# The causal mask of an attention block: a select on POOL after the sigmoid, in place of a product on PE before it

## The chip, the core and the metric

The kernel runs on one core of one Trainium2 chip. The time is the device time in microseconds from the launch's start to its end. PE is TensorE, ACT ScalarE, DVE VectorE, POOL GpSimd, and SP SyncE, which here only issues transfers. Each engine executes its own queue in order; a semaphore makes one engine wait for another.

## The reference, cut to what matters

One layer of a hybrid encoder: a projection, then stick-breaking attention (8 heads) beside an RWKV-7 recurrence, then an output projection and a feed-forward part, for 2048 prompt tokens and 32 sample tokens. The change is in the attention of the prompt:

```
z = q k^T / sqrt(64)                       # one row for each query t, one column for each key s
mask = s < t                               # strictly causal
log_1mb = where(mask, log_sigmoid(-z), 0)  # a masked key breaks nothing off: factor 1
after = reverse cumsum(log_1mb) - log_1mb
weight = where(mask, exp(log_sigmoid(z) + after), 0)
o = weight @ v
```

A key's weight is its sigmoid times the product of (1 - sigmoid) over all later keys before the query. A masked key must count as a factor of one in the running product.

## The kernel before

The kernel has three parts. The first projects all tokens and writes queries, keys and values to DRAM. The second, from about 943 to 1756 us of the profiled span, runs attention, recurrence and the first rows of the output projection interleaved. The third is the rest of the output projection and the feed-forward part.

Attention goes head by head, for each of four query blocks of 512 tokens (`qg`), through key blocks of 512 (`kc`) from the query's own block back to the first. In each pair of blocks there are four tiles of 128 queries (`j`). `scores` (lines 818 to 830) makes one tile: two products add up to the scores `z` in PSUM (queries and keys are split in a high and a low part), and in the query's own block, where `kc == qg`, only the first `n = (j + 1) * 128` keys are taken. The last 128 of these are the diagonal square. There a third product (line 827) adds `identr` times `mnegr`, that is 0 or -2^100, so that masked scores become hugely negative. `stick` (774 to 778) then makes the tile `R` in SBUF: a sigmoid of -z/8 on ACT gives the factor of each key, which is 1 where the score was masked, and a scan on DVE turns it, from the last key to the first, into running products. The scan takes its starting value from the key block treated before, and 1.0 in the own block. The scan's second operand is `z`, which it ignores, so a score buffer is free again only after the scan; there are three (`psZ`).

`turn` (832) transposes a tile's four squares on PE and splits them in high and low parts on ACT and DVE (`split`, line 103). `values` (844) multiplies them with differences of the values, which are held so that the running products can serve as weights. Transposes come four score tiles behind, and values two steps behind them.

The generators `attention`, `recurrence` and `first_rows` are drawn from by a loop with weights (line 1169), and a scheduling layer then sets each engine's order. POOL does little in this part: memsets of a recurrence tile (line 1028), powers and products of the group norm (983 to 989), and low parts of the output projection's operands (747). Each stands in POOL's queue and waits there for what it needs.

In this program 128 tiles have the mask product: 8 heads, 4 query blocks, 4 tiles each. The mask's constants are made once, at the start of part one (lines 92 to 94 and 180 to 185).

Of the kernel before, what the change touches and what calls it, by code (L numbers as in the profile page):

```python
# [10 lines left out]
F32R = mybir.dt.float32r  # L11
AF = mybir.ActivationFunctionType
ALU = mybir.AluOpType
# [4 lines left out]
P = 128  # L18
# [34 lines left out]
def kernel(ctx: ExitStack, tc: tile.TileContext, x_prompt, x_sample, cache_k, cache_v,  # L53
# [6 lines left out]
    PE, ACT, DVE, POOL, SP = nc.tensor, nc.scalar, nc.vector, nc.gpsimd, nc.sync  # L60
# [25 lines left out]
    ident = const.tile([P, P], F32, name="ident")  # L86
# [2 lines left out]
    POOL.memset(neghalf, -0.5)  # L89
    cab = ctx.enter_context(ExitStack())  # L90
    cp_ab = cab.enter_context(tc.tile_pool(name="cab", bufs=1))
    identr = cp_ab.tile([P, P], F32R, name="identr")
    POOL.tensor_copy(identr, ident)
    mnegr = cp_ab.tile([P, P], F32R, name="mnegr")
    mnegs = cp_ab.tile([P, TS], F32, name="mnegs")
    zr = cp_ab.tile([TS, 1], F32, name="zr")
    POOL.memset(zr, 0.0)
# [16 lines left out]
    with tc.tile_pool(name="pa0", bufs=1) as pe, tc.tile_pool(name="pa1", bufs=1) as pa, \  # L114
# [65 lines left out]
        mneg = pe.tile([P, MX + 2], F32, tag="df", name="mneg")[:, 0:P]  # L180
        POOL.memset(mneg, NEG)
        POOL.affine_select(mneg, mneg, [[1, P]], ALU.is_ge, 0.0, base=0, channel_multiplier=-1)
        POOL.tensor_copy(mnegr, mneg)
        for j in range(4):
            POOL.tensor_copy(mnegs[32 * j:32 * j + 32, :], mneg[0:32, 0:32])
        m64 = pe.tile([P, MX], mybir.dt.bfloat16, name="m64")
# [2 lines left out]
        for r in (0, 64):  # L189
            POOL.affine_select(mA[r:r + 64, 0:64], mA[r:r + 64, 0:64], [[1, 64]], ALU.is_gt, 0.0,  # L190
                               base=0, channel_multiplier=-1)
            POOL.affine_select(mA[r:r + 64, 64:128], mA[r:r + 64, 64:128], [[1, 64]], ALU.is_ge, 0.0,
                               base=0, channel_multiplier=-1)
# [69 lines left out]
        def superblock(sb, T0, NTILE):  # L263
# [154 lines left out]
            def g_k(w, c):  # L418
# [47 lines left out]
                def stage3(av, E65, Em, nrm):  # L466
                    rr = live["rr"]
                    kk = pe.tile([P, MX], F32, tag="kk", name="kk")
                    DVE.scalar_tensor_tensor(kk[:, 0:WT], kr[:, 0:WT], col(R_KK + c), nrm[:, 0:WT],
                                             ALU.mult, ALU.mult)  # L470
                    KB = pe.tile([P, 12, P], F32, tag="KB", name="KB")
                    QR = pe.tile([P, 12, P], F32, tag="QR", name="QR")
                    POOL.tensor_tensor(QR[:, 0:NC, 0:64], c3(kk), E65[:, 0:NC, 0:64], ALU.mult)
                    POOL.tensor_tensor(QR[:, 0:NC, 64:128], c3(rr), E65[:, 0:NC, 1:65], ALU.mult)
                    POOL.tensor_tensor(kk[:, 0:WT], kk[:, 0:WT], av[:, 0:WT], ALU.mult)
                    POOL.tensor_tensor(KB[:, 0:NC, 64:128], c3(kk), c3(Em), ALU.mult)
                    DVE.tensor_scalar(av[:, 0:WT], av[:, 0:WT], -1.0, col(R_KA + c), ALU.add, ALU.mult)
                    DVE.scalar_tensor_tensor(kr[:, 0:WT], av[:, 0:WT], 1.0, kr[:, 0:WT], ALU.add, ALU.mult)
                    POOL.tensor_tensor(KB[:, 0:NC, 0:64], c3(kr), c3(Em), ALU.mult)
                    DVE.scalar_tensor_tensor(rr[:, 0:WT], rr[:, 0:WT], col(R_RK + c), kr[:, 0:WT],  # L480
                                             ALU.mult, ALU.mult)
                    chunk_dst(lambda a, m: QR_d[a:a + m, c].rearrange("j p t -> p j t"), 0, NC,
                              lambda o, m: QR[:, o:o + m, :])
                    defer(3, lambda: scores(rr, KB, QR))
# [278 lines left out]
    with tc.tile_pool(reuse_waits="tile", name="bp", bufs=6) as bp, \  # L763
# [7 lines left out]
            tc.tile_pool(reuse_waits="tile", name="psX", bufs=1, space=PSUM) as psX:  # L771
        NB, LAG, LAG2, LOOK, RW = 12, 4, 2, 8, PAST + TS + 1

        def stick(z, R, n, before):

            ACT.activation(R[:, 0:n], z[:, 0:n], AF.Sigmoid, scale=-0.125)  # L776
            rv = R[:, 0:n][:, ::-1]
            DVE.tensor_tensor_scan(rv, rv, z[:, 0:n], before, ALU.mult, ALU.bypass)  # L778

# [8 lines left out]
        pieces, state = {}, {}  # L788
# [29 lines left out]
        def scores(h, qg, kc, j):  # L818

            k = pieces[h, kc][0]  # L820
            n = (j + 1) * P if kc == qg else 512
            z = psZ.tile([P, 512], F32, tag="z", name="z")
            js = slice(j * P, (j + 1) * P)
            PE.matmul(z[:, 0:n], state[h, qg][:, 0, js], k[:, 0:n], start=True, stop=False)  # L824
            PE.matmul(z[:, 0:n], state[h, qg][:, 1, js], k[:, 0:n], start=False, stop=kc != qg)  # L825
            if kc == qg:
                PE.matmul(z[:, n - P:n], identr, mnegr, start=False, stop=True)
            R = bk.tile([P, 512], F32, tag="R", name="R", bufs=NB)
            stick(z, R, n, 1.0 if kc == qg else state[h, qg, kc + 1, j][:, 0:1])
            state[h, qg, kc, j] = R  # L830

        def turn(h, qg, kc, kb):
# [91 lines left out]
        def attention():  # L924
            A, B, loads = [], [], []
            for hq, h in [(hq, h) for hq in range(2) for h in range(H)]:
                if hq == 0 and h == 2:
                    for kc in (2, 1, 0):
                        for e in range(2):
                            A.append((lambda kc=kc, e=e: s_scores(kc, e), 1.0 if kc == 2 else 3.0))  # L930
                        for e in range(2):
                            B.append((len(A) - 1, lambda kc=kc, e=e: s_turn(kc, e),
                                      lambda kc=kc, e=e: s_values(kc, e), 0.2 if kc == 2 else 2.0))
                for qg in (2 * hq, 2 * hq + 1):
                    for kc in range(qg, -1, -1):
                        loads.append((len(A), h, qg, kc))
                        for j in range(4):
                            n = (j + 1) * P if kc == qg else 512
                            A.append((lambda h=h, qg=qg, kc=kc, j=j: scores(h, qg, kc, j), 2 * n / 2400))
                        for kb in range(4):  # L940
                            m = 4 - (kb if kc == qg else 0)
                            B.append((len(A) - 1, lambda h=h, qg=qg, kc=kc, kb=kb: turn(h, qg, kc, kb),
                                      lambda h=h, qg=qg, kc=kc, kb=kb: values(h, qg, kc, kb),
                                      m * (0.107 + 2 * P / 2400)))
# [243 lines left out]
    with tc.tile_pool(reuse_waits="tile", name="c1", bufs=1) as cp, tc.tile_pool(reuse_waits="tile", name="psM", bufs=6, space=PSUM) as psM, \  # L1188
# [38 lines left out]
        with tc.tile_pool(reuse_waits="tile", name="co", bufs=2) as co:  # L1227
# [7 lines left out]
            for at, (i, dhs) in enumerate(tiles):  # L1235
                t0, n = halves[1][0][i]
# [20 lines left out]
        with tc.tile_pool(reuse_waits="tile", name="cz", bufs=3, side="right") as cz, \  # L1257
# [87 lines left out]
            for q in range(1, len(seq), 2):  # L1345
# [14 lines left out]
                hf, j = seq[q]  # L1360
# [31 lines left out]
```

## Time and profile before

| | us |
|---|---|
| median of 3 runs | 3440.98 (3435.89 to 3441.1) |
| the profiled execution | 3431.45 |
| its span, first to last instruction | 3429.6 |
| PE busy | 3258.3 (95%) |
| DVE busy | 1752.8 (51%) |
| ACT busy | 1151.4 (34%) |
| POOL busy | 861.8 (25%) |

The granted clock of PE averages 0.979 of 2.4 GHz. The busy shares are means over all three parts; what the change does has to be read in the second part alone, from 943 to 1756 us. A PE matmul's duration in a row is its run from first input to last output; the next one starts well before it ends.

### The profile page before, as it was taken

What the parts mean: (1) busy time and instruction counts of PE and PEld (TensorE: products, weight loads), DVE (VectorE), ACT (ScalarE), POOL (GpSimd) and SP (SyncE); (2) the same over time, 40 slices, a digit from 0 to 9 for tenths busy, and PEclk for the clock granted to TensorE, in tenths of its full rate; (3) what the DMA queues carried; (4) which work ended last, traced back from release to release, by engine and by line L of the source; (5) the groups of instructions that cost most, each with busy time, mean ns of one, the idle gap of its engine ahead of it and who ended that gap; (6) DMA issues with size and microseconds to landing.
All of it is one profiled execution on the core that took longest, in us unless ns stands there. A gap on an engine that the chain in (4) does not pass through costs nothing.

```text
span 3429.6 us, 50515 instructions
## 1 busy us (share of the span) xinstructions
PE 3258.3 (95%) x20281; PEld 2829.6 (83%) x20281; DVE 1752.8 (51%) x2449; ACT 1151.4 (34%) x2231; POOL 861.8 (25%) x719
## 2 busy tenths in 40 slices
PE   8998898889689999999999999999999999999998
PEld 7988898878677777877877989999899788888886
DVE  4675757678678888777853322222222322222223
ACT  6444343434155555454542311111112211111111
POOL 3332423253101121122223411212112321221121
PEclk9999999989889999999999999999999999999999
DMA  4555565565775655656643611111112411111111
GB/s 148 164 158 149 169 185 140 155 190 146 213 187 146 178 149 154 171 145 162 160 123 117 197 38 50 44 43 50 37 50 72 151 50 50 45 48 43 49 43 50
DMA packets 481762, 395.82 MB, mean 115 GB/s; under 512 B 72228, under 2 KB 403568, under 8 KB 481528
## 3 DMA queue, kind: packets, MB, share of 16 engines
q1 hardware_dynamic: 393000, 346.58, 35.5%
q10 hardware_dynamic: 88528, 46.02, 4.9%
q8 instruction: 160, 2.62, 0.3%
q14 instruction: 74, 0.61, 0.1%
HBM read 278.19 MB, written 114.31 MB: 114 GB/s over the span
## 4 chain that ended last, share of the span: by engine, by line
PE 50%; DVE 1%; DMA 0%; ACT 0%; issue 0%; POOL 0%; POOLq 0%; ACTq 0%; SPq 0%; DVEq 0%
PE gu L1305 29%; PE dn L1325 15%; PE mo L760 3%; PE wt L837 0%; PE pt L1221 0%; PE av L851 0%; PE av L852 0%; DVE R L778 0%; PE z L824 0%; PE sap L1104 0%; PE z L825 0%; PE snp L1113 0%; DMA mx<-mixT_d 0%; ACT yt L1213 0%; PE yp L1126 0%
## 5 line engine op out<-in xcount | busy, mean ns | idle before, releaser
L1328 DVE TENSOR_TENSOR x<-x,dn 128x512 f32<-128x512 f32 x374 | 255.7, 687 | 243.3 <-PE dn L1325 243.3
L778 DVE TENSOR_TENSOR_SCAN R<-R,z 128x512 f32<-128x512 f32 (+2 forms) x320 | 338.5, 1084 | 73.3 <-ACT R L776 70.8
L1305 PE MATMUL gu<-h2h,wh 128*128 128x352 f32 (+1 forms) x1760 | 368.4, 351 | 1.7 <-ACT wh L104 1.2
L1305 PE MATMUL gu<-h2h,wl 128*128 128x352 f32 (+1 forms) x1760 | 369.0, 351 | 0.0
L1305 PE MATMUL gu<-h2l,wh 128*128 128x352 f32 (+1 forms) x1760 | 367.3, 351 | 0.0
L1305 PEld LDWEIGHTS gu<-h2h,wh 128*128 128x128 f32 x1760 | 305.1, 188 | 33.9 <-ACT wh L104 1.4
L1305 PEld LDWEIGHTS gu<-h2l,wh 128*128 128x128 f32 x1760 | 305.3, 188 | 31.0
L1305 PEld LDWEIGHTS gu<-h2h,wl 128*128 128x128 f32 x1760 | 305.1, 188 | 30.2
L1325 PE MATMUL dn<-dh,hdh 128*128 128x512 f32 x748 | 295.1, 394 | 0.0
L1325 PE MATMUL dn<-dh,hdl 128*128 128x512 f32 x748 | 295.0, 394 | 0.0
L1325 PE MATMUL dn<-dl,hdh 128*128 128x512 f32 x748 | 293.8, 393 | 0.0
L324 PE MATMUL mm<-hh,wh 128*128 128x384 f32 (+4 forms) x1296 | 248.4, 333 | 2.5 <-ACT xp L336 1.2
L324 PE MATMUL mm<-hh,wl 128*128 128x384 f32 (+4 forms) x1296 | 234.8, 324 | 0.0
L324 PE MATMUL mm<-hl,wh 128*128 128x384 f32 (+4 forms) x1296 | 231.2, 320 | 0.0
L324 PEld LDWEIGHTS mm<-hh,wh 128*128 128x128 f32 (+1 forms) x1296 | 211.1, 192 | 9.7 <-ACT xp L336 1.6
L776 ACT ACTIVATE R<-z 128x512 f32<-128x512 f32 (+2 forms) x320 | 163.5, 535 | 159.0 <-PE z L825 98.2
L324 PEld LDWEIGHTS mm<-hh,wl 128*128 128x128 f32 (+1 forms) x1296 | 211.2, 190 | 2.6
L324 PEld LDWEIGHTS mm<-hl,wh 128*128 128x128 f32 (+1 forms) x1296 | 207.4, 186 | 2.6
L104 ACT CAST dh<-rawd 128x1024 fp32r<-128x1024 f32 x44 | 44.2, 1047 | 425.4 <-PE dn L1325 424.4
L105 DVE TENSOR_TENSOR wtl<-wt,wth 128x512 fp32r<-128x512 f32 (+1 forms) x320 | 178.9, 595 | 15.5 <-ACT wth L104 14.2
L104 ACT CAST wth<-wt 128x512 fp32r<-128x512 f32 (+1 forms) x320 | 156.0, 529 | 53.4 <-PE wt L837 51.1
L837 PE MATMUL wt<-ident,R 128*128 128x128 f32 x1088 | 162.6, 278 | 10.2 <-DVE wtl L105 9.3
(754 smaller groups left out, 5418.6 us busy)
## 6 DMA issues: line engine op xcount, KB each, us to landing
wraw<-in_w_in ACTq DMA_DIRECT2D x77, 512.0 KB
rawg<-in_w_gate SPq DMA_DIRECT2D x44, 512.0 KB
rawu<-in_w_up SPq DMA_DIRECT2D x44, 512.0 KB
rawd<-in_w_down SPq DMA_DIRECT2D x44, 512.0 KB
A_d<-a SPq DMA_DIRECT2D x28, 512.0 KB
mx<-mixT_d SPq DMA_DIRECT2D x27, 512.0 KB
k<-khl_d SPq DMA_DIRECT2D x42, 256.0 KB
vp<-vhl_d SPq DMA_DIRECT2D x42, 256.0 KB
```

What stands on the lines that cost most here:

```text
L104: ACT.copy(hi, src)
L105: (eng or DVE).tensor_tensor(lo, src, f32(hi), ALU.subtract)
L324: PE.matmul(ps[0:wd, 0:s1 - s0], a_[:, kt, 0:wd], b_[:, kt, s0:s1], start=i == 0, stop=i == 3 * KT - 1)
L760: PE.matmul(ps[0:n], a_[:, kt, 0:n], b_[:, kt, :], start=j + kt == 0, stop=j == 2 and kt == KT - 1)
L776: ACT.activation(R[:, 0:n], z[:, 0:n], AF.Sigmoid, scale=-0.125)
L778: DVE.tensor_tensor_scan(rv, rv, z[:, 0:n], before, ALU.mult, ALU.bypass)
L837: PE.transpose(pt[:, j * P:(j + 1) * P], state[h, qg, kc, j][:, kb * P:(kb + 1) * P], ident)
L1305: PE.matmul(ps[:, 0:n], a_[:, kt, :], b_[:, kt, s0:s1], start=i == 0, stop=i == 23)
L1325: PE.matmul(ps[0:n], a_[:, i * P:i * P + n], b_[:, ds_], start=k == 0, stop=k == 3 * len(js) - 1)
L1328: DVE.tensor_tensor(x1[:n, ds_], x1[:n, ds_], ps[0:n], ALU.add)
```

## The change

The mask product on PE and its two constants go. In a query's own block, after the sigmoid, POOL replaces the masked entries of the last 128 columns by 1.0 with an affine select (kept where query minus key minus 1 is at least 0). The sigmoid and the scan read `z` as before.

```diff
-    identr = cp_ab.tile([P, P], F32R, name="identr")
-    POOL.tensor_copy(identr, ident)
-    mnegr = cp_ab.tile([P, P], F32R, name="mnegr")
...
-        POOL.tensor_copy(mnegr, mneg)
...
-        def stick(z, R, n, before):
+        def stick(z, R, n, own, before):
             ACT.activation(R[:, 0:n], z[:, 0:n], AF.Sigmoid, scale=-0.125)
+            if own:
+                POOL.affine_select(R[:, n - P:n], R[:, n - P:n], [[-1, P]], ALU.is_ge, 1.0, base=-1, channel_multiplier=1)
             rv = R[:, 0:n][:, ::-1]
             DVE.tensor_tensor_scan(rv, rv, z[:, 0:n], before, ALU.mult, ALU.bypass)
...
-            PE.matmul(z[:, 0:n], state[h, qg][:, 1, js], k[:, 0:n], start=False, stop=kc != qg)
-            if kc == qg:
-                PE.matmul(z[:, n - P:n], identr, mnegr, start=False, stop=True)
+            PE.matmul(z[:, 0:n], state[h, qg][:, 1, js], k[:, 0:n], start=False, stop=True)
             R = bk.tile([P, 512], F32, tag="R", name="R", bufs=NB)
-            stick(z, R, n, 1.0 if kc == qg else state[h, qg, kc + 1, j][:, 0:1])
+            stick(z, R, n, kc == qg, 1.0 if kc == qg else state[h, qg, kc + 1, j][:, 0:1])
```

The order on PE in the last diagonal block (head 7, last 512 queries), before; `z` are scores, `wt` transposes, `av` values, `mo` the output projection:

```order
L851 MATMUL av<-wth,vp 128x512
L852 MATMUL av<-wtl,vp 128x512
L824 MATMUL z<-k,q 128x384
L825 MATMUL z<-k,q 128x384
L827 MATMUL z<-mnegr,identr 128x128
L824 MATMUL z<-k,q 128x512
L825 MATMUL z<-k,q 128x512
L827 MATMUL z<-mnegr,identr 128x128
L837 MATMUL wt<-ident,R 128x128 x8
```

The same place now (line numbers are lower by three or four):

```order
L848 MATMUL av<-wth,vp 128x512
L849 MATMUL av<-wtl,vp 128x512
L823 MATMUL z<-k,q 128x384
L824 MATMUL z<-k,q 128x384
L823 MATMUL z<-k,q 128x512
L756 MATMUL mo<-woh,mh 128x512 x8
L756 MATMUL mo<-wol,mh 128x512 x8
L824 MATMUL z<-k,q 128x512
```

The mask products are gone, and the scheduling layer has moved sixteen products of the output projection to between the two products of the last score tile.

POOL's queue at the same block, before; `Yt` and `lnst` are the group norm, `mx` operands of the output projection, `TTt` the recurrence's tile:

```order
L988 TENSOR_TENSOR Yt<-Yt,gl 128x512
L989 TENSOR_TENSOR Yt<-Yt,ge 128x512
L747 TENSOR_TENSOR mx<-mx,mh 128x1024 x2
L1028 MEMSET TTt 32x512
L983 TENSOR_SCALAR lnst<-lnst 128x8
L984 TENSOR_TENSOR lnst<-lnst,neghalf 128x8
```

The same place now:

```order
L985 TENSOR_TENSOR Yt<-Yt,gl 128x512
L986 TENSOR_TENSOR Yt<-Yt,ge 128x512
L775 AFFINE_SELECT R<-R 128x128 x2
L743 TENSOR_TENSOR mx<-mx,mh 128x1024
L775 AFFINE_SELECT R<-R 128x128 x2
L1025 MEMSET TTt 32x512
L743 TENSOR_TENSOR mx<-mx,mh 128x1024
L980 TENSOR_SCALAR lnst<-lnst 128x8
L981 TENSOR_TENSOR lnst<-lnst,neghalf 128x8
```

The four selects of the block stand among POOL's other work: two of them before a subtraction of the output projection, and two behind it.

## Rows read from the trace of the kernel before

**Rows 1.** Busy time by engine, 943 to 1756 us (instruction counts, clock, DMA behind).

```profile
943.00:1756.00 813.00, 775.64 (x6715) 630.00 (x6716) 657.93 (x887) 435.30 (x927) 151.52 (x125) 0.98 0.60 158
```

**Rows 2.** Lines 827 and 824: durations min/median/max; idle before line 824 by releaser.

```profile
L827 PE MATMUL z<-mnegr,identr x128: 218/225/415, 944.1 to 1718.7; 128*128 128x128 f32 x128
...
  DVE R L778: 21.9, 45
```

**Rows 3.** DVE's groups in that stretch: busy, mean ns, idle before.

```profile
L778 DVE TENSOR_TENSOR_SCAN R<-R,z 128x512 f32<-128x512 f32 (+2 forms) x320 | 338.5, 1084 | 73.3 <-ACT R L776 70.8
L105 DVE TENSOR_TENSOR wtl<-wt,wth 128x512 fp32r<-128x512 f32 (+3 forms) x312 | 173.8, 593 | 10.3 <-ACT wth L104 9.1
```

**Rows 4.** Timeline of the first diagonal blocks: start, duration, engine, idle before.

```profile
946.86 0.79 PE L824 MATMUL z<-k,q 128*128 128x512 f32 x1 [0.83 <-DVE R L778]
...
952.04 0.28 ACT L776 ACTIVATE R<-z 128x128 f32<-128x128 f32 x1 [3.22 <-PE z L827]
952.35 0.42 DVE L778 TENSOR_TENSOR_SCAN R<-R,z 128x128 f32<-128x128 f32 x1 [2.28 <-ACT R L776]
```

**Rows 5.** Chain of waits, 1681.5 to 1719.5 us: summary, then start and duration.

```profile
by line: PE mo L760 25.5%; PE wt L837 16.7%; PE av L851 7.6%; PE av L852 6.8%; PE z L824 6.5%; DVE R L778 6.5%; PE up L1094 5.7%; PE z L825 5.5%; ACT ob L857 3.0%; PE snp L1113 2.8%; PE sap L1104 2.8%; PE z L827 1.9%; PE mps L1050 1.9%; DVE
...
1681.70 0.26 PE z L827
...
1706.11 2.45 DVE R L778 x2
...
1715.64 0.11 PE z L827
...
1718.85 0.06 PE z L827
```

**Rows 6.** Timeline at the start: selects on POOL, and DVE beside them.

```profile
5.75 0.29 POOL L182 TENSOR_SCALAR_AFFINE_SELECT mneg<-mneg 128x128 f32<-128x128 f32 x1
...
8.76 2.48 DVE L140 SCALAR_TENSOR_TENSOR xt<-xt,rstd,gb 128x1024 f32<-128x1024 f32 x2 [6.14 <-DMA gb<-in_norm_mix_g]
...
11.38 0.24 POOL L190 TENSOR_SCALAR_AFFINE_SELECT mA<-mA 64x64 f32<-64x64 f32 x1
11.54 1.22 DVE L105 TENSOR_TENSOR wl<-wraw,wh 128x1024 fp32r<-128x1024 f32 x1 [0.30 <-ACT wh L104]
11.57 1.29 POOL L192 TENSOR_SCALAR_AFFINE_SELECT mA<-mA 64x64 f32<-64x64 f32 x1
```

**Rows 7.** Timeline at 18 to 20 us: from ACT to POOL to DVE.

```profile
18.70 0.19 ACT L134 ACTIVATION_READ_ACCUMULATOR junk<-xt 128x1 f32 x1
18.98 0.19 POOL L109 TENSOR_SCALAR ss<-ss 128x1 f32<-128x1 f32 x1 [4.89 <-ACT junk L134]
19.25 0.56 POOL L110 TENSOR_TENSOR rstd<-ss,neghalf 128x1 f32<-128x1 f32 x1
19.84 1.28 DVE L140 SCALAR_TENSOR_TENSOR xt<-xt,rstd,gb 128x1024 f32<-128x1024 f32 x1 [1.55 <-POOL rstd L110]
```

**Rows 8.** Timeline: a sigmoid whose scan is not due, and the last diagonal pair.

```profile
1219.86 0.28 ACT L776 ACTIVATE R<-z 128x128 f32<-128x128 f32 x1 [0.50 <-PE z L827]
1221.50 1.28 DVE L778 TENSOR_TENSOR_SCAN R<-R,z 128x512 f32<-128x512 f32 x1
...
1718.38 1.17 ACT L776 ACTIVATE R<-z 128x384 f32<-128x384 f32 x2 [0.70 <-PE z L827]
1718.90 2.06 DVE L778 TENSOR_TENSOR_SCAN R<-R,z 128x384 f32<-128x384 f32 x2 [0.39 <-ACT R L776]
```

**Rows 9.** POOL's costliest group, 943 to 1756 us: busy, mean ns, idle before.

```profile
L747 POOL TENSOR_TENSOR mx<-mx,mh 128x1024 fp32r<-128x1024 f32 x16 | 39.6, 2475 | 68.6 <-ACT mh L746 68.4
```

**Rows 10.** Timeline, 1680 to 1684 us: a diagonal sigmoid while POOL is busy.

```profile
1680.74 2.74 POOL L747 TENSOR_TENSOR mx<-mx,mh 128x1024 fp32r<-128x1024 f32 x1 [4.81 <-ACT mh L746]
1682.35 0.55 ACT L776 ACTIVATE R<-z 128x128 f32<-128x128 f32 x2
1682.66 1.00 DVE L778 TENSOR_TENSOR_SCAN R<-R,z 128x128 f32<-128x128 f32 x2
```

## The prediction, made before the result was known

> **What bounds the kernel now.** The change touches one stretch only: the attention blocks, from the first score product at 943 us to the last one at about 1756 us. I read that stretch first, as a sum over one window [rows 1]. PE is busy 775.64 of 813 us there, DVE 657.93 (81%), POOL 151.52 (19%). PE is the engine that is nearly full. DVE is second, and close enough that it sometimes decides. After the stretch comes the feed-forward part, which this change does not touch, so what is won or lost in the stretch is carried to the end as it is.
>
> Second, the view of one line: who held up the score products. PE sat idle before line 824 until a scan on DVE had freed a score buffer for 21.9 us in 45 places [rows 2]. There are 320 score tiles, so a scan holds PE up in 45/320 = 14% of them. The other way round, the scans' row of the stretch [rows 3] says that DVE waited 70.8 us for sigmoids. So PE and DVE hand the lead to each other, and PE has it most of the time.
>
> Third, the chain of waits over the last two diagonal blocks of the stretch, 1681.5 to 1719.5 us [rows 5]. The PE lines that its summary row names add up to 84% of that time, DVE's scan to 6.5%. All eight mask products of those two blocks lie on the chain. None of their eight scans does: the only scans on it are the two at 1706.11, which belong to later key blocks without a mask.
>
> **What the change removes.** 128 matmuls with their weight loads: 8 heads x 4 query blocks x 4 row tiles [rows 2]. The row of line 827 gives a median of 225 ns for one, but that is its run through the array; what counts is how long the next matmul is held back. The chain shows that directly: 0.26, 0.06, 0.06, 0.06, 0.11, 0.06, 0.06, 0.06 us for its eight pieces, 0.73 us together, 0.091 us each (the first, the fifth and the last stand in [rows 5]). The long ones stand where the next weight load has no long matmul to hide behind. So the removed work is 128 x 0.091 = 11.7 us if all of it were on the path; at 0.06 it would be 7.7 us. I take 11.7 and keep PE's share of the chain, 84%: a gain of 9.8 us. The rest vanishes where PE waits for a scan right behind the removed product.
>
> The Trainium skill, "TensorE: Matmul & The Clock Gate", section "LDWEIGHTS (loading the stationary operand)", has a weight load take its columns divided by 1.2 in ns, which is 107 ns for these 128 columns whatever else runs. By that the removed slots would be 128 x 0.107 = 13.7 us and the gain 11.5 us. The trace agrees only for the slot of 0.11 us; six of the eight slots are 0.06 us, where the load hides.
>
> Two casts on POOL at the start go too. DVE's first work on the tokens waits until 8.76 us for a load, not for POOL [rows 6], so I cost them at nothing. Uncovered, two copies of the size of the select at 5.75 us (0.29 us) would be 0.6 us.
>
> **What it adds.** 128 selects on POOL, each between a sigmoid on ACT and the scan of the same tile on DVE. The trace has a select of exactly this shape, 128x128 in place: 0.29 us [rows 6]. From ACT's end to POOL's start it is 0.09 us (18.89 to 18.98), from POOL's end to DVE's start 0.03 us (19.81 to 19.84) [rows 7]. The hop from ACT to DVE that falls away is 0.03 us (952.32 to 952.35) [rows 4]. So a scan may start 0.29 + 0.09 + 0.03 - 0.03 = 0.38 us later after its sigmoid than now. The sigmoid itself starts earlier by the removed slot, 0.06 to 0.11 us. Net: 0.3 us.
>
> Whether that costs anything depends on what DVE does meanwhile. I set each of the 128 diagonal sigmoids beside its scan. In 64 the scan starts less than 0.3 us after the sigmoid's end, mostly 0.03 us: DVE is idle or just free (an early pair is at 952.04 and 952.35, the last two at 1718.38 and 1718.90) [rows 4, 8]. In the other 64 DVE is still busy with older work: the sigmoid at 1219.86 ends at 1220.14, and at 1221.50 DVE still starts an older, longer scan [rows 8]. There the select is free. Over the 64 exposed ones the missing time adds up to 14 us on DVE.
>
> Next, POOL's queue. POOL executes in order, and a select waits behind what stands before it: above all the sixteen subtractions of 2.48 us [rows 9], but also the group norm's work and memsets that themselves wait for PE. At 18 of the 128 sigmoid ends POOL is busy now, for another 0.9 us on average; one is at 1682.35, where a subtraction runs from 1680.74 to 1683.48 and the scan now starts at 1682.66 [rows 10]. That adds 16 us, so DVE is delayed by about 30 us in all, spread over a stretch in which it is idle for 813 - 658 = 155 us. In the new order the memsets that wait for PE stand, but for a few, behind PE work that is older than the next tile's score product, so I add nothing for them.
>
> What is queued behind a waiting scan on DVE: the next scans, the low parts of the weights (line 105), and the recurrence's copies (lines 1096, 1118); PE waits for these. Only where PE is already close behind does the delay reach it. The first four diagonal blocks (943 to 973 us, 16 tiles, 11 of them exposed) are such a place: at 946.86 PE waits 0.83 us for the scan [rows 4]. There I let the whole 0.3 us through, 11 x 0.3 = 3.3 us. Of the remaining 27 us I let through the 14% in which a scan holds PE up: 3.8 us. Bounds for this term: nothing, if DVE makes it up everywhere as it does at the two blocks of rows 5, and all 30 us. I take 3.3 + 3.8 = 7 us, nearer to the low end, since the chain's rows are the only ones that show what ended last, and they show the scans off it.
>
> **The sum.** -9.8 + 7 = about -3 us. The profiled execution took 3431.45 us (span 3429.6 and 1.85 us around it), so it would come out at 3428.5 us. The median of the runs shown is 3440.98 us, 9.5 us above the profiled one, so by the same step it goes to 3438 us. That is 0.09%, and about 0.2% (7 us) is what a measurement here can tell from no change. The order also moves pieces of the recurrence and of the output projection between the score products; I price that at zero, plus or minus 5 us.
>
> **Rivals.**
> Full gain, selects hidden everywhere: the 11.7 us come through, DVE makes up its delay in its 155 us of idle time. For it: rows 5, eight of eight products on the path and no scan. Against it: the 45 places where a scan does hold PE [rows 2]. Time: 3440.98 - 11.7 = 3429 us.
>
> Slower, by POOL's queue: selects stand behind the subtractions of rows 9 and the rest of POOL's work, scans start late, and PE runs out of its three score buffers. Price: all 30 us reach PE, 9.8 - 30 = 20 us slower, 3461 us. It turns the sign once a third of the 30 us gets through (9.8/30), and is slower by 0.2% from 56% on ((9.8 + 7)/30). For it: DVE at 81%, in-order queues. Against it: POOL is idle 81% of the stretch, and half the scans have time to spare.
>
> Slower, by POOL held up while DVE works: at 11.57 a 64x64 select took 1.29 us, ending when DVE's subtraction of two SBUF operands (11.54 to 12.76) ended; the same size took 0.24 us at 11.38 with DVE idle [rows 6]. If every select were stretched like that to 1.3 us, the exposed time would rise from 14 to 91 us, and by the 14% of rows 2 some 11 us more would reach PE: 8 us slower, 3449 us. Against it: in the stretch nearly all of DVE's work is scans and low parts, which read one operand from PSUM [rows 3]. The Trainium skill, "SBUF — State Buffer", section "Who interferes with whom", says just this: a DVE instruction with two SBUF inputs contends with a GpSimd instruction that reads SBUF, one with at most one does not. By that rule few selects are stretched. The trace agrees at 11.38 and 11.57; no row of before shows a select beside a scan.
>
> The change doesn't do what it says: the products' slots were free time, and the scans cost nothing either: 3441 us, inside "no difference".
>
> **How the numbers follow.** Forecast, within 0.2%: 0.54 (with the case of free slots). Full gain: 0.28. POOL's queue: 0.14. Stretched selects: 0.04. So faster 0.28, same 0.54, slower 0.18. The range runs from 3426 us (full gain, and 3 us for the new order) to 3450 us (the queue letting through some 60%): it leaves out most of the queue's case and a little on the fast side, about 2 in 10.
>
> **What would show it.** Right: no line with the mask product; selects of 0.3 us; the idle time before the scans now ended by POOL, some 15 to 30 us more than before; PE's idle time before score products up by 5 to 10 us; the stretch shorter by 0 to 8 us. Wrong: selects of 0.7 us and more beside scans; PE waiting for scans well over 40 us in all; or the stretch longer with PE's waits unchanged, which would point to the moved order.

## The result, and the profile after

The changed kernel takes 3464.23 us (median of 4 runs, 3460.37 to 3466.57) where the kernel before took 3438.43 us beside it. The ratio is 1.0076, with a 95% interval from 1.0061 to 1.0091: **about 26 us, 0.8%, slower**. The prediction had said 3438 us and "no difference", with 3450 us as its upper end.

The loss lies in the attention stretch alone. The first score product starts at 945.3 us (943.7 before), and by the last one the lag is 34 us. The feed-forward part then runs as before: its first and its last products both come 33.8 us later than in the profiled run of before. (That run took 3431.45 us at a mean clock of 0.979, less than the median of before, whose mean clock over all its runs is 0.9757; by the medians the lag is 26 us.)

Busy time by engine in the stretch, to be held against [rows 1]. The columns are the same: the window, its length, busy time and instruction count of each engine, granted clock, share and rate of the DMA.

```profile
943.00:1790.00 847.00, 789.04 (x6578) 619.99 (x6579) 660.13 (x887) 439.82 (x926) 187.41 (x253) 0.97 0.59 152
```

The window is 34 us longer. PE has 128 products fewer in it and is yet busy for 13 us longer, 789.04 us for 775.64, at a lower mean clock; the other 21 us are idle time of PE, 58 us for 37. POOL has 36 us more to do, which are the selects. DVE has what it had.

The select's own line: duration in ns as min/median/max.

```profile
L775 POOL TENSOR_SCALAR_AFFINE_SELECT R<-R x128: 284/294/872, 949.6 to 1752.6; 128x128 f32<-128x128 f32 x128
```

The scans' line, as far as it answers to [rows 3]: what ended DVE's idle time ahead of a scan.

```profile
  POOL R L775: 46.1, 27
  ACT R L772: 17.6, 23
```

Before, 70.8 us of this idle time were ended by the sigmoid; now 46.1 + 17.6 = 63.7 us by both. So the selects did not make DVE idle for longer in sum, and they are as short as the prediction took them (294 ns). Next, PE ahead of the first score product of each tile, which answers to [rows 2]:

```profile
  DVE R L777: 59.4, 88
```

That is 59.4 us in 88 places, where it was 21.9 us in 45. This view adds up two records of the engine, its weight loads (PEld) and its products (PE), and a load can wait while an earlier product still runs. Taken apart (us in total, times, longest), before:

```profile
PE z L824 <- DVE R L778: 6.7, 17, 0.8
PEld z L824 <- DVE R L778: 15.2, 28, 1.1
```

and now:

```profile
PE z L823 <- DVE R L777: 19.5, 32, 3.2
PEld z L823 <- DVE R L777: 39.9, 56, 3.7
```

So the products themselves waited 6.7 us before and 19.5 us now. Below, the sum of both records is used to compare kernels; it is not time that PE lost. An early wait, at the first tiles, where no scan can run ahead (start, duration, engine, line; the idle time before in brackets):

```profile
949.56 0.95 POOL L775 TENSOR_SCALAR_AFFINE_SELECT R<-R 128x128 f32<-128x128 f32 x3 [20.26 <-ACT R L772]
949.88 1.84 DVE L777 TENSOR_TENSOR_SCAN R<-R,z 128x128 f32<-128x128 f32 x3 [18.05 <-POOL R L775]
950.36 0.29 PEld L823 LDWEIGHTS z<-k,q 128*128 128x128 f32 x1 [3.74 <-DVE R L777]
```

By itself this picture fits the rival in which selects delay the scans and the scans PE. But the scheduler had also moved the order of some three thousand instructions, which the prediction priced at "zero, plus or minus 5 us". The two are not to be told apart in this one trace.

### The profile page after: what moved, and what is told of

Same layout as the page of the kernel before. It is cut to its first block, busy times and chain, and to the rows that moved or that the text cites. A ratio compares the mean times of both kernels' runs of the same rounds, so it can differ in the third digit from the quotient of the medians.

```text
span 3462.2 us, 50711 instructions
## 1 busy us (share of the span) xinstructions
PE 3273.1 (95%) x20153; PEld 2821.9 (82%) x20153; DVE 1756.0 (51%) x2449; ACT 1156.2 (33%) x2231; POOL 900.0 (26%) x845
## 4 chain that ended last, share of the span: by engine, by line
PE 70%; DVE 12%; issue 7%; POOL 3%; DMA 3%; ACT 3%; SPq 1%; ACTq 0%; POOLq 0%; DVEq 0%
PE gu L1302 29%; PE dn L1322 14%; PE mm L320 8%; PE mo L756 5%; DVE R L777 2%; PE wt L834 2%; DVE t L543 1%; DVE Ti L545 1%; PE av L849 1%; PE av L848 1%; DVE wtl L102 1%; PE z L823 1%; PE sap L1101 1%; PE snp L1110 1%; PE z L824 1%
## 5 line engine op out<-in xcount | busy, mean ns | idle before, releaser
L777 DVE TENSOR_TENSOR_SCAN R<-R,z 128x512 f32<-128x512 f32 (+2 forms) x320 | 337.7, 1084 | 65.9 <-POOL R L775 46.1
L834 PE MATMUL wt<-ident,R 128*128 128x128 f32 x1088 | 174.2, 284 | 15.4 <-DVE wtl L102 13.9
L101 ACT CAST wth<-wt 128x512 fp32r<-128x512 f32 (+1 forms) x320 | 158.7, 527 | 70.8 <-PE wt L834 66.9
```

The costliest lines, as they stand in the source:

```text
L101: ACT.copy(hi, src)
L834: PE.transpose(pt[:, j * P:(j + 1) * P], state[h, qg, kc, j][:, kb * P:(kb + 1) * P], ident)
```

## The experiments

**How they are read.** A table in the kernel can put every engine's instructions into the order of another kernel. It ties each instruction behind the one ahead of it on its engine, in issue order alone, without a wait (shortened here):

```diff
+    for r in ORDER:                       # ranks, in the order of the other kernel
+        for i in [own[r]] + follow[r]:    # follow: what the other kernel doesn't have
+            add_manual_dep(i, last[i.engine].name, NoSync)
+            last[i.engine] = i
```

So content (product, select, both, neither) and order (old, new, others) can be set apart. Three more words: the **old order** is that of the kernel before, the **new order** that of the changed kernel, and a **score tile** is one of the 320 pairs of score products with what follows from it.

Each run gives a span S and a mean granted clock c. TensorE's clock has two levels, 1.2 and 2.4 GHz, so the time at the lower one is 2 x (1 - c) x S, and it costs up to half of itself, since PE is busy for some 95% of the span. What is left, c x S, is called the **work side** here (work and waits at the full clock), the other (1 - c) x S the **clock side**. In before the work side is 3352.6 us with a standard deviation of 2.9 us over its runs, the span 3436.1 us with 3.7. How much of the clock side shows in the span is less sure: a straight line through the 97 runs of before gives 0.6 us of span for each us of it, and 1.05 us when the clock side is fitted to the span instead. At less than 1 the work side comes out too low for a kernel with much time at 1.2 GHz, so the spans have to be read beside it. Means over 4 to 12 runs of each kernel, 97 of before:

| content, order | ratio to before, 95% | mean span us | clock | at 1.2 GHz, us | work side us |
|---|---|---|---|---|---|
| product, old (before) | 1 | 3436.1 | 0.9757 | 167 | 3352.6 |
| select, new (after) | 1.0076 (1.0061 to 1.0091) | 3462.1 | 0.9740 | 180 | 3372.1 |
| select, old (sel_ob) | 1.0035 (1.0022 to 1.0049) | 3448.7 | 0.9717 | 195 | 3351.1 |
| product, new (prod_oa) | 1.0060 (1.0048 to 1.0072) | 3457.2 | 0.9748 | 174 | 3370.1 |
| both, old (both_ob) | 1.0026 (1.0017 to 1.0034) | 3444.8 | 0.9747 | 174 | 3357.7 |
| neither, old (none_ob) | 0.9993 (0.9984 to 1.0001) | 3433.0 | 0.9744 | 176 | 3345.0 |
| neither, its own (none) | 1.0048 (1.0032 to 1.0064) | 3454.9 | 0.9732 | 185 | 3362.1 |
| both, its own (both) | 1.0003 (0.9994 to 1.0013) | 3439.7 | 0.9762 | 163 | 3358.0 |
| neither, order of both (none_bo) | 1.0005 (0.9995 to 1.0014) | 3436.3 | 0.9729 | 186 | 3343.2 |
| select, order of both (sel_bo) | 1.0051 (1.0039 to 1.0064) | 3451.7 | 0.9693 | 212 | 3345.8 |
| the same again (sel_bo2) | 1.0049 (1.0034 to 1.0064) | 3452.1 | 0.9687 | 216 | 3344.0 |
| select and idle product, same order (idle_prod) | 1.0010 (0.9998 to 1.0022) | 3438.5 | 0.9763 | 163 | 3357.1 |

### Order or select

Two theories: the moved order costs the 26 us, or the select's place between sigmoid and scan does. Four kernels cross them. The edits of the last two, each in the old order:

```diff
  # both_ob: the product stays, the select is added
+            if own:
+                POOL.affine_select(R[:, n - P:n], R[:, n - P:n], [[-1, P]], ALU.is_ge, 1.0, ...)
  # none_ob: neither
-                PE.matmul(z[:, n - P:n], identr, mnegr, start=False, stop=True)
```

> The changed kernel's work (selects, no product), but with every engine's instructions queued in the order of the kernel before; each select stands on POOL behind the instruction that the old order has ahead of its sigmoid. Theory order (the scheduler's moved pieces cost the 26 us): 3429 us, the old time less the 10 us of TensorE work that is gone. Theory latency (a select stands between sigmoid and scan, and score buffers come free later): 3464 us, as the changed kernel. Waits of the first score product for scans: near 22 us by order, near 59 us by latency.

> The old work (the product on TensorE, no selects) with every engine's instructions queued in the order of the changed kernel; each mask product stands right behind its second score product. Theory order: 3464 to 3474 us, the changed kernel's time and up to 10 us for the product. Theory latency: 3438 us, as the kernel before, with the waits of the first score product for scans back near 22 us.

> The old order with the product kept and the select put between sigmoid and scan as well (it sets to one what is one already). Theory latency: 3464 to 3474 us, since only the select's delay is added. Theory order: 3438 to 3445 us, since the order is the old one.

> The old order without any mask: neither product nor select, so the attention's diagonal blocks are not masked; what the product alone costs on the path. By the sum of the prediction 3428 us (10 us less than before). If the product lies in slots that TensorE has free anyway: 3438 us. Both theories expect the same here.

Measured: sel_ob 3449.81 us, prod_oa 3459.24, both_ob 3446.53, none_ob 3435.25, beside 3438.69 for before. Neither theory has it alone. The new order costs 0.60% without a single select in it; the selects cost 0.26% in the old order where the product stays. On the work side: the order 3370.1 - 3352.6 = **17.5 us**, the select 3357.7 - 3352.6 = **5.1 us** (or 3351.1 - 3345.0 = 6.1 without the product), the product's loss 3345.0 - 3352.6 = **-7.6 us**. With the select in it the new order costs 3372.1 - 3351.1 = 21.0 us. So -7.6 + 6.1 + 21.0 = 19.5 us, and the time at 1.2 GHz grows from 167 to 180 us, which is half of 13, 6.3 us: 26 us in all.

By the spans alone the shares are others, and they depend on the order of the steps. Product out, select in, new order: -3.1 + 15.7 + 13.4 = 26.0 us. New order first, then product out and select in: 21.1 + 4.9 = 26.0 us. So the order is worth 13 to 21 us of the 26; the edit without the moved order costs 12.6 us (sel_ob), and 4.9 us when both kernels have the new order. In none_ob, at 3435.25 us between its two expected times, the product's removal gives 3 us of time at most.

PE's wait for scans at the first score product goes the same way. In prod_oa, with no select:

```profile
  DVE R L812: 44.7, 71
```

In sel_ob, with the selects and the old order, it is 49 places:

```profile
  DVE R L811: 31.8, 49
```

So the new order alone takes it from 45 places to 71, the selects alone from 48 (29.2 us, none_ob) to 49 (31.8 us).

### What moved the order

The scheduler places instructions by its own reckoning of how long each takes. Was it the missing product or the added select that moved them? I let it make its own order for neither (none), for both (both), and for a third way to mask (fold, fold_ob): the mask goes into the scan as its second operand, so that neither product nor select is left.

```diff
-            DVE.tensor_tensor_scan(rv, rv, z[:, 0:n], before, ALU.mult, ALU.bypass)
+            if own:
+                DVE.tensor_tensor_scan(rv, rv, ones[:, 512 - n:512][:, ::-1], before, ALU.mult, ALU.max)
+            else:
+                DVE.tensor_tensor_scan(rv, rv, z[:, 0:n], before, ALU.mult, ALU.bypass)
```

> No mask at all, so the attention's diagonal blocks are not masked, in the scheduler's own order (173 score blocks without other work ahead of them, runs of up to eight). Theory order, with the lost product as its cause: 3455 us, 20 us over the same kernel in the old order (3435). Theory select: 3435 us.

> The product kept and the select put in as well, in the scheduler's own order, which stays near the old one (159 score blocks without other work ahead, runs of up to six). Theory order: 3447 us, as the same kernel in the old order, since only the select's own cost of about 9 us is left. Theory select (that the select in the scheduler's reckoning moves the order): 3460 us or more.

> The same mask in the scan, with the scheduler's own order. In that order 188 score blocks follow the one ahead of them with no other TensorE work between (164 in the old order, 174 in the changed kernel's) and there are more runs of seven and eight such blocks. Theory order (score blocks that stand closer make TensorE wait for scans): 3455 us or more, 20 us over the same kernel in the old order, though no select is in it. Theory select: 3435 us, equal to the same kernel in the old order.

> The mask moved into the scan itself: on diagonal blocks the running product is taken as max(factor x state, mask), the mask a constant tile of ones and zeros in place of the ignored score operand, so there is neither the product on TensorE nor a select on POOL, and the score buffer is free after the sigmoid; every engine's instructions queued in the order of the kernel before. If the select's hop is what cost 12 us in the old order: 3435 us, as without any mask. If a scan with this operand on a diagonal block is dearer than 1.06 us on average, more by 128 times the difference as far as it shows.

Measured: none 3454.85 us, both 3441.27, fold 3486.24, fold_ob 3446.16, beside 3440.31 for before. **It is the missing product.** With no select anywhere, the scheduler's order for "neither" costs 3362.1 - 3345.0 = 17.1 us of work side over the old one, as the new order does; with product and select together its order costs nothing over the old one (3358.0 and 3357.7; the time is 5 us less, and 6 us under the expected 3447). Fold shows it at its largest: 1.0134 (1.0115 to 1.0152) in its own order, 1.0013 (1.0001 to 1.0025) in the old one, twice the loss that was expected. What the orders have in common can be counted on PE: the score tiles that follow the one ahead of them with less than 0.3 us of other PE work (recurrence, output projection) between. They are 164 in the old order, 159 in that of both, 174 in the new one, 173 in none, 186 in fold. The longest run of such tiles behind the first 24 is 6 tiles in the old order and 10 in the new one. Many pieces of the recurrence and the projection stand two to five score tiles later than before. The reading is that without the product a tile looks shorter to the scheduler, so that it packs the tiles closer and the work that stood between them comes later; the scheduler's own reckoning was not looked at. Nor does the count rank the orders: the half order prod_h1, further down, has 163 such tiles, with a longest run of 10, and costs 0.56%. On fold_ob I was wrong by 8 us (0.9989 of before expected, 1.0013 measured); the last section comes back to it. PE's wait ahead of score products in none:

```profile
  DVE R L774: 47.1, 71
```

### Why the closer order costs time

If tiles that stand close make PE wait for DVE, then the new order should be almost free where DVE has little to do. The pair cuts every scan to 128 columns (and leaves the mask out), in the old and the new order.

```diff
-            rv = R[:, 0:n][:, ::-1]
-            DVE.tensor_tensor_scan(rv, rv, z[:, 0:n], before, ALU.mult, ALU.bypass)
+            rv = R[:, n - P:n][:, ::-1]
+            DVE.tensor_tensor_scan(rv, rv, z[:, n - P:n], before, ALU.mult, ALU.bypass)
```

> No mask, and every attention scan cut to its first 128 columns (the rest of the running product is left out), in the old order: VectorE has some 250 us less to do, so that a score product seldom waits for a scan. Serves as the base of the next run; 3435 us or less (same TensorE work as without the mask), 3415 us if all its waits for scans and splits go.

> The same cut scans (the rest of the running product left out, no mask) in the changed kernel's order. If the moved order costs its 17 to 20 us because score blocks that stand closer wait for VectorE's scans: within 7 us of the same kernel in the old order. If it costs them in another way (weight loads, the recurrence finishing late, the output projection): 17 to 20 us more than the same kernel in the old order.

Measured: 3398.46 and 3411.05 us. The 12.6 us between them lie outside both expectations. On the two sides it reads better: the work side is 3320.7 and 3326.1 us, so the new order costs 5.4 us there (17.5 with whole scans); the time at 1.2 GHz is 156 and 167 us, another 5.5. PE's waits for scans are nearly gone, in the old order and in the new one:

```profile
  DVE R L808: 3.7, 2
```

```profile
  DVE R L808: 9.8, 13
```

So some 12 of the 17.5 us go away when DVE has less to do, and about 5 us (with four runs of each, give or take 5) don't; of the spans' 21.1 us, 10.7 are left. That points to waits for DVE as the larger part of what the order costs. The traces book only a part of it as idle time of PE: from 943 to 1925 us that is 43.1 us in before and 53.8 in prod_oa, 10.7 us more, 7.8 of them ended by DVE, where the score products fall 24 us behind. What makes up the rest stays open. The base itself, light_ob, came out 17 us below its lowest expected time. The second pair asks where: the new order up to the 200th score tile and the old one behind it (prod_h1), and the reverse (prod_h2), with the product.

> The old work (product, no select) in the changed kernel's order up to the 200th of the 320 score blocks and in the old order from there on. By the steps seen in the trace of the same work in the changed kernel's order (9 us behind at block 200, 24 at the end): 3447 us if the lag so far stays and nothing follows. If the loss is all in the later half, with its more and longer runs of score blocks that stand close: 3438 us.

> The old order up to the 200th score block, the changed kernel's from there on, with the product. By the same steps: 3453 us (15 of the 24 us come behind block 200). If the loss is all in the first half: 3438 us. The two halves should add up to the whole order's 20 us if each piece costs its own.

Measured: 3456.61 and 3449.46 us beside 3436.6: ratios 1.0056 (1.0044 to 1.0068) and 1.0036 (1.0024 to 1.0048), together more than the whole order's 0.60%. The first is 10 us over its dearer expectation, the second between its two. The work sides are 3361.5 and 3367.4 us, 8.9 and 14.8 over before, which is what the trace's steps had given (9 and 15). What spoils the sum of the times is the clock side, 185 us at 1.2 GHz in the one and 159 in the other. The order loses time all along, not in one place.

### What the select costs, and by what

Is it POOL's time or the place between sigmoid and scan? In aside_ob the 128 selects work on a tile of their own. In zfree_ob the scan's ignored operand is the tile itself, so that a score buffer need not wait for a scan that waits for a select.

```diff
  # aside_ob
-                POOL.affine_select(R[:, n - P:n], R[:, n - P:n], [[-1, P]], ALU.is_ge, 1.0, ...)
+                POOL.affine_select(aside, aside, [[-1, P]], ALU.is_ge, 1.0, ...)
  # zfree_ob
-            DVE.tensor_tensor_scan(rv, rv, z[:, 0:n], before, ALU.mult, ALU.bypass)
+            DVE.tensor_tensor_scan(rv, rv, rv if own else z[:, 0:n], before, ALU.mult, ALU.bypass)
```

> No mask; 128 selects of the same size run on POOL on a tile of their own, which nothing waits for and which wait for nothing (the diagonal blocks are not masked), in the old order. If the select costs 12 to 15 us in the old order by standing between sigmoid and scan: 3436 us, as without any mask. If it is POOL's time or its port: 3447 to 3450 us.

> The changed kernel's work in the old order, but on diagonal blocks the scan's ignored operand is the running product's own tile, so the score buffer comes free with the sigmoid and no longer with the scan behind the select. If the select costs its 12 us by holding score buffers: 3436 to 3440 us. If by VectorE coming later to everything: 3448 to 3450 us.

Measured: aside_ob 3437.18 us, 0.9994 of before (0.9986 to 1.0003), against 0.9993 with no select: POOL's time costs nothing, the place costs. The scans of sel_ob show how, by what ended DVE's idle time before them:

```profile
  POOL R L809: 60.7, 39
  ACT R L806: 35.0, 30
```

In none_ob it was 70.0 us, all behind the sigmoid. So the selects made DVE idle for 60.7 + 35.0 - 70.0 = 26 us more.

zfree_ob took 3470.26 us, 1.0095 (1.0081 to 1.0110), slower than either expectation, with 222 us at 1.2 GHz; its work side is 3353.9 us, 2.8 above sel_ob, so most of the difference is on the clock side. Its profile shows the quickest of the five executions (3449.29 us at a clock of 0.976; the others took 3467 to 3475 us at 0.965 to 0.968), so what slowed the others isn't in it. In that execution PE's wait for scans did fall, from 31.8 to 23.7 us,

```profile
  DVE R L811: 23.7, 48
```

but a new cost came in: six scans with both operands in SBUF, each beside a subtraction on POOL, took 0.8 to 2.2 us longer than others of their length, 7.1 us together. The longest one, in the two timelines of zfree_ob at 1634 us, DVE's and POOL's (start, duration):

```profile
1634.51 3.42 DVE L811 TENSOR_TENSOR_SCAN R<-R 128x512 f32<-128x512 f32 x1 [1.37 <-POOL R L809]
```

```profile
1634.45 2.40 POOL L777 TENSOR_TENSOR mx<-mx,mh 128x1024 fp32r<-128x1024 f32 x1
```

So whether held score buffers are what the select costs isn't settled: the test changed two things.

### The clock

The order of both is a good one for product and select together (1.0003). It should have been good for the changed kernel's work too.

> The changed kernel's work (selects, no product) in the order that the scheduler makes for product and select together. If the order made in sight of the product is the right one for this work: 3436 to 3439 us (the 3441 us of product and select together, less 2 to 5 us for the product). If the select costs 12 us in any order in which TensorE has the product's time back: 3448 us.

> No mask (the diagonal blocks are not masked), in that same order. If the select is nearly free in this order: 3434 to 3438 us, within 3 us of the run with selects. If it costs 12 us here as well: 3436 us, with the selects at 3448.

Measured: sel_bo 3453.0 us beside 3436.6, none_bo 3434.78 (by the ratios, 1.0051 and 1.0005). Taking the product out of this order made it some 12 us **slower**, though the work side fell from 3358.0 to 3345.8. What rose was the time at 1.2 GHz, from 163 to 212 us. The last pair put that to the test on one chip: the same kernel, and beside it one with a product of the same size in the old product's place that adds zeros.

```diff
-        POOL.tensor_copy(mnegr, mneg)
+        POOL.tensor_tensor(mnegr, ident, ident, ALU.subtract)
```

> Select on POOL as in the changed kernel, and in the place of the old product one of the same size that adds zeros (it masks nothing), in the order made for product and select together: 128 x 0.091 us = 11.7 us more TensorE work than the next run. If TensorE's clock falls less often while it has this work: 3438 to 3442 us, some 10 us faster than the next run, and some 40 us less at the lower clock. If TensorE's work simply adds: 3455 us or more.

> The changed kernel's work in the same order, without that product. If the clock is what costs: 3450 to 3455 us as on the other chip. If the earlier difference was one between chips: 3436 to 3442 us.

Measured: 3441.44 us with the idle product, 3453.72 without. PE has 13 us more on its work side (3357.1 and 3344.0) and 53 us less at 1.2 GHz (163 and 216): the useless work makes the kernel 12 us faster. The clock records of the two traces show where: in the stretch TensorE is at 1.2 GHz for 92 us in sel_bo2 and 29 us in idle_prod, ahead of it for 117 and 122 us. One such place in the profiled runs: first sel_bo2, from 1317 us (columns as in [rows 1]; the clock is the third number from the end):

```profile
1317.00:1322.00 5.00, 3.65 (x31) 2.56 (x30) 3.86 (x7) 1.08 (x2) 0.00 (x0) 0.99 1.06 298
1322.00:1332.00 10.00, 10.00 (x60) 7.82 (x58) 5.99 (x7) 4.40 (x8) 3.06 (x3) 0.50 0.27 80
```

and idle_prod:

```profile
1317.00:1322.00 5.00, 4.55 (x47) 3.70 (x48) 3.87 (x5) 2.75 (x5) 0.57 (x2) 1.00 0.90 246
1322.00:1332.00 10.00, 10.00 (x95) 8.16 (x94) 8.85 (x12) 6.46 (x16) 2.52 (x2) 1.00 0.16 37
```

In sel_bo2 PE was idle for 1.35 us between 1317 and 1322 us, and in the next 10 us it ran 60 matmuls at a granted 0.50, where idle_prod ran 95 at 1.00. The wait alone is not the difference. It stands in both, ahead of the same product, between 1300 and 1325 us (us in total, times, longest):

```profile
PE mps L1081 <- DVE Us L1127: 1.3, 1, 1.3
```

```profile
PE mps L1086 <- DVE Us L1132: 1.3, 1, 1.3
```

In sel_bo2 the clock falls 2 us behind this wait, in idle_prod it stays up. What in the work around it decides this stays open.

The Trainium skill, "TensorE: Matmul & The Clock Gate", section "Part 1: The HAM clock gate", says that the clock follows how busy PE has recently been. The table agrees: in each of the five pairs that differ by the product alone, the one without it spends more time at 1.2 GHz (176 for 167, 195 for 174, 180 for 174, 212 and 216 for 163 us; the third difference alone is not clear of noise).

None of these versions beats the kernel before. Of those that compute the whole, both (1.0003) and idle_prod (1.0010) come nearest.

## Why the prediction was wrong

**The step that failed is the last sentence of the sum**: "The order also moves pieces of the recurrence and of the output projection between the score products; I price that at zero, plus or minus 5 us". The order costs 17 to 21 us on the work side and 13 to 22 us of span (prod_oa, none against none_ob, after against sel_ob). It wasn't chance either, since each of the three orders made without the product lost time; that score tiles stand closer than DVE can follow is what the short scans point to. Two numbers that should have warned were in the prediction: DVE busy for 81% of the stretch, and PE held up by scans already. The second was misread. Its 45 places are 28 waits of weight loads and 17 of products, so a scan held up the product of 17 in 320 tiles, 5% and not 14%. With 5% the sum would have been 2 us lower, further from the result.

**The second fault is a term that is not there**: the clock. The prediction reckoned a removed product as PE time gained. In a fixed order its removal gained 3 us of mean span at best (none_ob), and cost 4 us (both_ob to sel_ob) and 5 us (prod_oa to after), neither clear of noise, and 12 to 14 us (the order of both). In all three the kernel holds the selects. The sum has no row for that, although [rows 1] showed a mean clock of 0.98 in the stretch, below 1.

**What held.** The removed slots: 9.8 us expected, 7.6 measured on the work side (0.059 us for one; 3.1 us of span for all). The select: 0.29 us expected, 0.294 measured; hop from ACT 0.09 expected, a median of 0.068 measured; hop to DVE 0.03 and 0.033. DVE's delay: about 30 us expected, 26 measured in the old order. What of it reaches PE: 7 us expected, 5.1 and 6.1 measured on the work side (2.6 in the order of both, 3345.8 - 3343.2). Selects stretched by DVE: three of 128, to 721, 732 and 872 ns, 1.4 us together; the two groups of [rows 3] are 78% of DVE's work, not nearly all of it. So the sum of the terms that were worked out, -3 us, comes out at -1.5 us on the work side of sel_ob (3351.1 - 3352.6). In time it doesn't hold: the selects cost 8.7 us of span with the product and 15.7 without, and sel_ob is 12.6 us slower than before, with 195 us at 1.2 GHz for 167. The split puts that down to the clock; at 0.6 us of span for each us of the clock side, sel_ob would be 4 us of work over before, and the selects would cost 6.5 to 10 us. So the near agreement on the work side leans on the split, and in time the sum was wrong about the edit as well.

**The rivals.** The time came out near that of "POOL's queue" (3461), but not by it. In the trace of after 15 of the 128 selects start more than 0.2 us after their sigmoid, and their excess over a free hop is 12 us, less than the 16 expected. The free slots came nearest to a truth: the slot gave work time back, and the clock took much of it. No rival named the order.

**The signs.** "PE waiting for scans well over 40 us in all" was listed as a sign against the forecast, which it was (59.4), but the text took it for the queue's sign and a longer stretch "with PE's waits unchanged" for the order's. The order does its harm through those very waits (44.7 us in prod_oa, without any select). A sign is worth something only if the rivals differ in it.

## What to carry to other kernels

Where a scheduler reckons durations, an edit that shortens one engine's step also re-spaces everything around it. Pin the old order and measure the edit alone, and then the new order with the old work in it; what the new order does to the waits for the second busiest engine is a first price, and counting steps that now stand close is not enough. Work taken off an engine that waits often is not all gained: read the time at the lower clock next to the span, in both kernels, before you believe a saving or blame a stall.

## What the runs showed of the hardware

TensorE work of no use made the kernel faster: 128 idle products added 13 us to the work side and took 53 us off the time at 1.2 GHz (3441.44 us against 3453.72). A wait of PE of 1.3 us was followed by a fall of the clock in the one kernel and not in the other. What exactly lets the clock fall was not tried.

A scan that took 1.23 us at the median with both operands in SBUF, and 1.27 us with the second in PSUM, took 3.42 us in zfree_ob when both its operands lay in SBUF and a POOL subtraction of 2.40 us had started 0.06 us ahead of it. In fold_ob's trace eleven scans beside POOL subtractions were stretched by 0.3 to 1.9 us, 10.2 us together; no scan with its second operand in PSUM passed 1.283 us in before, none_ob, sel_ob or after. That is likely a part of why fold_ob missed its expected 3435 us: its work side is 2.6 us over none_ob's (3347.6 and 3345.0), its time at 1.2 GHz 189 us for 176. The Trainium skill, "SBUF — State Buffer", section "Who interferes with whom", has it so: DVE with two SBUF inputs and GpSimd reading SBUF share a port under an exclusive lock. The prediction had applied this rule to the selects: the three that were stretched stood beside DVE instructions with two inputs in SBUF. It held up scans for longer.
